# A decoder layer with mLSTM and memory attention on one core: weights of the last MLP chunk kept, memory input moved, root columns reordered, chunk steps spread, sums moved

## The chip, the cores and the metric

The kernel runs on one core of a Trainium2 chip. TensorE (PE in the profile) multiplies matrices; VectorE (DVE), ScalarE (ACT) and GpSimd (POOL) work element by element; SyncE (SP) issues the DMA transfers. Each engine takes its instructions in the order in which they stand in its queue and waits for semaphores that the others set. The metric is the time of one execution on the device in microseconds (us): the median of several runs.

## The reference

The input x has 1024 tokens of width 1024, the memory has 256 rows. One layer is computed, then a last RMSnorm (gains, weights and biases are parameters):

```
h     = rms_norm(x, norm_mix0)
qk, v, o_pre, i_pre, f_pre, q_mem = split(h @ w_in)      # 768, 768, 768, 4, 4, 256 columns
q, k  = split(silu(causal_conv4(qk, w_conv)))            # 4 heads of 96
y_ml  = rms_norm(mlstm(q, k, v, i_pre + b_i, log_sigmoid(f_pre + b_f)), w_hnorm) * sigmoid(o_pre)
mem_k, mem_v = split(rms_norm(mem, mem_norm) @ w_mem_kv)
y_mem = softmax(q_mem @ mem_k^T / 8) @ mem_v             # 4 heads of 64, 256 memory rows
x     = x + concat(y_ml, y_mem) @ w_out
x     = x + square(relu(rms_norm(x, norm_ffn0) @ w_ff1)) @ w_ff2   # 4096 hidden
out   = rms_norm(x, final_norm)
```

The mLSTM keeps a matrix state C for each head (96 x 192) and runs in chunks of 128 tokens with stabilised exponential gates: in a chunk, n = (q k^T * weights) v + q C; then C = decay * C + (k * u)^T v.

## The kernel before

**Products.** Every operand of a product in float32 is split into a high part of fewer bits and a low part, the rest. A product is three matmuls into the same PSUM bank (mm3, L110 high by high, L111 high by low, L112 low by high). `load_w` (L93) brings a weight: SP's DMA into a raw tile (4 of them), a cast on ACT for the high part (L88 or L91), a subtraction on POOL for the low part (L103). The results lie in a ring "w" of 5, or in another pool if one is given.

**Stages.** The tokens go in two halves (512 each), with d_model on the partitions. The work is written as Python generators: `run(dense, side, every)` issues a step of the dense work, and after every `every`-th step one step of the side work. L681 to L692 hold the plan: project_qk(0) (768 columns over 8 blocks of input) with the zeros of the memory's block matrices beside it; project_v(0) (two halves of four token tiles, 8 blocks each) with `memory_load`, which loads, scales, splits and squares the memory's rows (tile xm); then the query of the memory, the memory's keys and values (`memory_kv`), with the gates of the mLSTM beside it; project_o(0) with the memory's scores (tiles: softmax quotients pr L597, transposed by PE as ct L607); then project_qk(1) and project_v(1) with the chunks of the first half (`mlstm_chunk`, two yields each: s, k; n, c; the rest) after every second step; and so on.

**Roots.** An RMSnorm's sum of squares over partitions is a product with a matrix of ones (ssq, L142); two transpositions on DVE (L144, L150) with POOL's power between give the inverse roots as a row for each token (rr), and `rms_cols` copies them as a column (rk, four copies on DVE, L188). After project_qk's products DVE evacuates their banks with the factor rr (L285); convolutions follow (ACT L243, DVE L246, ACT L253 as tile ct, DVE L254).

**MLP.** Most of it runs in pairs of blocks with sums of weights. The last quarter of w_ff2 is direct, `last_chunk` (L1218): pass 0 makes 8 output blocks for the first half of the tokens (512 columns), two more passes make them for 256 tokens each of the second half (tok1, tok2). Every block is added to the residual (L1241), squared on ACT (L1244) and its square added on DVE (L1247, kept for the next block by `lag`). `root_first` sums them over partitions by PE (L159), and begins the root with ACT; `root_last` ends it on DVE; `write` multiplies and stores.

**What sets the order.** A scheduler with a simulated timeline orders each engine's queue when the kernel is built, within the data's dependences and the buffers; `keep_in_program_order` and `issue_after` bind single instructions. So the code's order moves what stands ahead of what on an engine, and the order in the queues has to be read from the built program.

## Time and profile before

| what | value |
|---|---|
| median of 3 runs | 1064.99 us (1062.97 to 1065.62) |
| profiled execution: its own time | 1062.4 us |
| its span, first to last instruction | 1060.7 us |
| mean granted TensorE clock | 0.993 |
| busy: PE, DVE, ACT, POOL | 1035.6, 696.7, 545.5, 592.7 us (98, 66, 51, 56%) |
| HBM read, written | 114.52, 36.19 MB, 142 GB/s over the span |

The busy time of an engine is the time in which one of its instructions ran. PE has hardly any free time in the whole span; the other three have much, but not in every stage. A row of a timeline has the start, the duration, the engine, the line, the operation, the output and its inputs, the count where rows of one kind are joined, and in brackets the idle time just before and what ended it.

### The profile page before, as it was taken

To read this page: it belongs to the slowest core of one execution; us is meant where nothing else is said; L and a number is where in the kernel's file an instruction comes from. 1 tells how busy PE (TensorE), PEld (TensorE's weight loads), DVE (VectorE), ACT (ScalarE), POOL (GpSimd) and SP (SyncE) were. 2 spreads that over 40 slices of the span, in tenths; PEclk is the share of its full clock that TensorE was granted. 3 is DMA by queue.
4 is the path that set the end of the run, shared out by engine and by line. 5 is a ranking of instruction groups with operands and counts; after the bars stand their busy time and mean duration, and the time that the engine had idled before them with its cause. 6 is when DMAs were issued, how large, how long until landed. Compare 5 with 4: busy or idle time off the path is not lost.

```text
span 1060.7 us, 14584 instructions
## 1 busy us (share of the span) xinstructions
PE 1035.6 (98%) x5018; PEld 887.1 (84%) x5018; DVE 696.7 (66%) x1122; ACT 545.5 (51%) x1050; POOL 592.7 (56%) x448
## 2 busy tenths in 40 slices
PE   9989999999999999999999999999999999999996
PEld 7988998899998888877888888887778888888885
DVE  6596885952766457996534433434899888878557
ACT  7464773344754354465665565555454433443273
POOL 6755435554424475004755566565568787776455
PEclk9999999999999999999999999999999999999999
DMA  7443333232324466326555453437775545544124
GB/s 223 115 126 109 115 122 87 69 93 89 99 60 120 151 190 196 100 65 215 198 186 184 155 189 134 172 120 239 258 212 174 158 142 167 152 137 139 54 78 158
DMA packets 81802, 152.46 MB, mean 144 GB/s; under 512 B 8096, under 2 KB 26560, under 8 KB 80192
## 3 DMA queue, kind: packets, MB, share of 16 engines
q1 hardware_dynamic: 81584, 151.51, 45.5%
q8 instruction: 39, 0.64, 0.3%
q14 instruction: 35, 0.29, 0.1%
q10 hardware_dynamic: 144, 0.03, 0.0%
HBM read 114.52 MB, written 36.19 MB: 142 GB/s over the span
## 4 chain that ended last, share of the span: by engine, by line
PE 73%; DVE 8%; DMA 6%; issue 5%; POOL 5%; ACT 3%; SPq 0%; DVEq 0%; POOLq 0%; ACTq 0%
PE fX L110 5%; PE fX L112 5%; PE fX L111 5%; DMA hr<-hd 4%; PE gX L112 3%; PE gX L111 3%; PE gX L110 3%; PE wo L110 3%; PE wo L112 3%; PE wo L111 3%; PE fZ L111 2%; PE fZ L110 2%; PE fZ L112 2%; PE o L110 2%; PE o L111 2%
## 5 line engine op out<-in xcount | busy, mean ns | idle before, releaser
L116 DVE TENSOR_TENSOR hb<-hr,hb 128x1024 fp32r<-128x1024 f32 x53 | 88.5, 1670 | 9.1 <-ACT hb L115 8.9
L1142 DVE TENSOR_TENSOR xo<-xo,gX 128x512 f32<-128x512 f32 x112 | 74.3, 682 | 26.9 <-PE gX L112 22.8
L111 PE MATMUL gX<-hb,w_b 128*128 128x512 f32 x224 | 87.3, 390 | 1.6 <-DVE hb L116 1.6
L110 PE MATMUL gX<-hb,w_b 128*128 128x512 f32 x224 | 86.4, 391 | 0.5 <-ACT hb L115 0.4
L112 PE MATMUL gX<-hb,w_b 128*128 128x512 f32 x224 | 85.5, 391 | 1.0 <-POOL w_b L797 1.0
L91 ACT ACTIVATE w_b<-S_b 128x512 fp32r<-128x512 f32 x56 | 34.9, 628 | 75.4 <-PE gX L112 33.5
L115 ACT ACTIVATE hb<-hr 128x1024 fp32r<-128x1024 f32 x53 | 55.8, 1053 | 32.4 <-DMA hr<-hd 32.0
L103 POOL TENSOR_TENSOR w_wo<-r_wo,w_wo 128x512 fp32r<-128x512 f32 x32 | 45.4, 1425 | 48.4 <-ACT w_wo L91 47.0
L797 POOL TENSOR_TENSOR w_b<-r_b,w_b 128x512 fp32r<-128x512 f32 x42 | 68.5, 1644 | 5.9 <-ACT w_b L91 5.9
L748 POOL TENSOR_TENSOR S_b<-r_b,r_b 128x512 f32<-128x512 f32 x28 | 44.9, 1605 | 32.7 <-DVE w_b L797 27.1
L797 POOL TENSOR_TENSOR w_a<-r_a,w_a 128x512 fp32r<-128x512 f32 x30 | 39.4, 1312 | 38.3 <-ACT w_a L88 37.5
L103 POOL TENSOR_TENSOR w_v<-r_v,w_v 128x388 fp32r<-128x388 f32 x32 | 39.5, 1245 | 31.9 <-ACT w_v L91 31.8
L103 POOL TENSOR_TENSOR w_o<-r_o,w_o 128x384 fp32r<-128x384 f32 x32 | 33.5, 1054 | 41.2 <-ACT w_o L91 41.2
L103 POOL TENSOR_TENSOR w_qk<-r_qk,w_qk 128x384 fp32r<-128x384 f32 x32 | 38.5, 1218 | 26.8 <-ACT w_qk L91 26.8
L110 PE MATMUL fX<-xa,w_a 128*128 128x512 f32 x128 | 50.1, 391 | 1.5 <-ACT hq L1004 1.2
L111 PEld LDWEIGHTS gX<-hb,w_b 128*128 128x128 f32 x224 | 42.1, 188 | 10.8 <-DVE hb L116 2.2
L110 PE MATMUL wo<-xa,w_wo 128*128 128x512 f32 x128 | 51.0, 400 | 0.0
L112 PEld LDWEIGHTS gX<-hb,w_b 128*128 128x128 f32 x224 | 42.1, 188 | 10.5 <-POOL w_b L797 1.8
L110 PEld LDWEIGHTS gX<-hb,w_b 128*128 128x128 f32 x224 | 41.9, 188 | 10.6 <-DVE xo L1142 1.0
L111 PE MATMUL wo<-xa,w_wo 128*128 128x512 f32 x128 | 50.1, 391 | 0.0
L112 PE MATMUL wo<-xa,w_wo 128*128 128x512 f32 x128 | 50.0, 390 | 0.0
L111 PE MATMUL fX<-xa,w_a 128*128 128x512 f32 x128 | 49.9, 389 | 0.0
(396 smaller groups left out, 3450.2 us busy)
## 6 DMA issues: line engine op xcount, KB each, us to landing
hr<-hd SPq DMA_DIRECT2D x53, 512.0 KB, 3.7
r_b<-w_ff SPq DMA_DIRECT2D x56, 256.0 KB, 3.0
hd<-hq SPq DMA_DIRECT2D x54, 256.0 KB, 2.0
hd<-hq SPq DMA_DIRECT2D x12, 1024.0 KB, 4.1
r_a<-w_ff SPq DMA_DIRECT2D x36, 256.0 KB, 2.7
r_wo<-w_out SPq DMA_DIRECT2D x32, 256.0 KB, 2.7
r_a<-w_ff SPq DMA_DIRECT2D x13, 512.0 KB, 4.6
r_v<-w_v SPq DMA_DIRECT2D x32, 194.0 KB, 2.4
```

Source lines behind the costliest of these rows:

```text
L91: st["first_part"] = A.activation(dst, src, AF.Copy).ins
L103: i = engine.tensor_tensor(w[:, 1, :n], raw[:, :n], w[:, 0, :n], ALU.subtract)
L110: keep(T.matmul(out, lhsT=lh, rhs=rh, start=start, stop=False, skip_group_check=goes_on))
L111: keep(T.matmul(out, lhsT=lh, rhs=rl, start=False, stop=False, skip_group_check=goes_on))
L112: keep(T.matmul(out, lhsT=ll, rhs=rh, start=False, stop=stop, skip_group_check=goes_on))
L115: A.activation(hi, src, AF.Copy)
L116: V.tensor_tensor(lo, src, hi, ALU.subtract)
L748: i = (on or (V if both is not None and sums_on_v and key != "S4" else G)).tensor_tensor(t, x, y, op)
L797: low = engine.tensor_tensor(w[:, 1], src, w[:, 0], ALU.subtract)
L1142: V.tensor_tensor(x, x, banks[e], ALU.add)
```

## The change

The change has five parts. (1) `memory_load` moves from project_v(0) to project_qk(0), where its steps alternate with those of the zeros (a new generator `turns`), from the sixth step on; project_v(0) runs alone, and the first weight of the memory's query is no longer loaded ahead. (2) In `memory_kv` the four copies of the root as a column are issued behind the last subtraction that makes the keys. (3) The first half's chunks take a step after every third step of project_qk(1), then after every second of project_v(1). (4) In `last_chunk` the weights are loaded and split once, in pass 0, and kept for the second half's passes; those of output blocks 4 to 7 lie in the pool of the squared activations. (5) In the pass tok2 the squares of blocks 4 to 7 are not added on DVE, but go one by one into PE's sum; the sum for tok1 is issued between the products of block 4 and of block 5.

```diff
--- before.py
+++ after.py
@@ -211,6 +211,16 @@
     def seq(*gens):
         for g in gens:
             yield from g
+
+    def turns(*gens):
+
+        gens = list(gens)
+        while gens:
+            for g in list(gens):
+                if next(g, gens) is gens:
+                    gens.remove(g)
+                else:
+                    yield
 
 
     att = ExitStack()
@@ -342,21 +352,13 @@
                     f()
             yield
 
-    def query_weight(h, b, u):
-        return load_w(a["w_qm"][b, u], 512, f"qm{h}{b}{u}")
-
-    def query_ahead():
-
-        st["qm_w", 0, 0, 0] = query_weight(0, 0, 0)
-        yield
-
     def project_qmem(h):
         qm = mem.tile([P, 2, 2, HT], F32R, tag="qm", name=f"qm{h}")
         st["qm", h] = qm
         for b in range(2):
             p = ps(f"qm{h}{b}")
             for u in range(2):
-                w = st.pop(("qm_w", h, b, u), None) or query_weight(h, b, u)
+                w = load_w(a["w_qm"][b, u], 512, f"qm{h}{b}{u}")
                 for kk in range(4):
                     k = 4 * u + kk
                     c = slice(kk * P, (kk + 1) * P)
@@ -410,8 +412,7 @@
                     mm3(p[:, :NMEM], w[:, 0, cc], w[:, 1, cc], xm[:, k, 0], xm[:, k, 1], k == 0, k == KB - 1)
                 if (b, u) == (1, 0):
                     parts = wpool.tile([P, 2, 512], F32R, tag="w", name="sums_m", bufs=5)
-                    rbc, c = rms(acc, NMEM, "m", [parts[:, i] for i in range(2)])
-                    rk = rms_cols(c, NMEM, "m")
+                    rbc, cols = rms(acc, NMEM, "m", [parts[:, i] for i in range(2)])
                 yield
         for b, p in enumerate(pk):
             t = at.tile([P, HT], F32, tag="cacc", name=f"mkt{b}", bufs=2)
@@ -420,7 +421,8 @@
                 rows = slice(64 * e, 64 * e + 64)
                 own = slice(NMEM * e, NMEM * e + NMEM)
                 A.activation(kbd[rows, b, 0, own], t[rows, :NMEM], AF.Copy)
-                V.tensor_tensor(kbd[rows, b, 1, own], t[rows, :NMEM], kbd[rows, b, 0, own], ALU.subtract)
+                keys_made = V.tensor_tensor(kbd[rows, b, 1, own], t[rows, :NMEM], kbd[rows, b, 0, own],
+                                            ALU.subtract).ins
         pv = [ps(f"mv{t}") for t in range(2)]
         for u in range(4):
             w = load_w(a["w_mv"][u], 512, f"mv{u}")
@@ -433,6 +435,8 @@
                         k == 0, k == KB - 1)
             if u < 3:
                 yield
+        with tc.issue_after(keys_made):
+            rk = rms_cols(cols, NMEM, "m")
         for t in range(2):
             s = at.tile([P, HT], F32, tag="cacc", name=f"mvt{t}", bufs=2)
             V.tensor_scalar(s[:, :NMEM], pv[t][:, :NMEM], rk[:, t:t + 1], None, ALU.mult)
@@ -678,13 +682,15 @@
 
     chunks = lambda h: seq(*(mlstm_chunk(h, t) for t in range(TPH)))
 
-    run(project_qk(0), seq(wait(3), memory_zeros()))
+    run(project_qk(0), seq(wait(5), turns(memory_load(), memory_zeros())))
     nc.sync.dma_start(gbias, a["gbias"].partition_broadcast(P))
     nc.sync.dma_start(whn, a["whn"].partition_broadcast(P))
-    run(project_v(0), seq(memory_load(), wait(4), query_ahead()))
+    run(project_v(0))
     run(seq(project_qmem(0), memory_kv()), seq(wait(3), gates(0)))
     run(project_o(0), tiles(0))
-    run(seq(project_qk(1), project_v(1)), chunks(0), every=2)
+    steps = chunks(0)
+    run(project_qk(1), steps, every=3, finish=False)
+    run(project_v(1), steps, every=2)
     rest = seq(gates(1), tiles(1), chunks(1))
     run(seq(project_qmem(1), project_o(1, lambda k: transpose_y(0, k))), rest, finish=False)
     run(project_out(0, lambda k: transpose_y(1, k)), rest)
@@ -1268,16 +1274,17 @@
                     keep(i)
             nc.sync.dma_start(out[h, :, b:b + 2, tok], o)
 
-        def weights(h, b):
+        def weights(b):
+
             for j in range(2):
-                ws[b, j] = load_w(a["w_ff2"][c, b // 2 % 2, b // 4, j], 512, f"f2{b}{j}{h}", fp if h and b > 3 else None)
+                ws[b, j] = load_w(a["w_ff2"][c, b // 2 % 2, b // 4, j], 512, f"f2{b}{j}", fp if b > 3 else None)
 
 
         tok = slice(0, HT)
         acc = cm.tile([P, HT], F32, tag="acc", name="oacc0")
         for b in range(KB):
             if b % 2 == 0:
-                weights(0, b)
+                weights(b)
             p = ps(f"f2{b}0")
             products(0, b, tok, p, 0)
             add(x1[0][:, b, tok], p, acc, b == 0, f"0{b}")
@@ -1287,7 +1294,6 @@
         tok1 = slice(0, HQ)
         acc1 = cm.tile([P, HT], F32, tag="acc", name="oacc1")
         for b in range(0, KB, 2):
-            weights(1, b)
             p = ps(f"f2{b}1")
             for e in range(2):
                 products(1, b + e, tok1, p, e * HQ)
@@ -1309,26 +1315,36 @@
         tok2 = slice(HQ, HT)
         acc2 = cm.tile([P, HT], F32, tag="acc", name="oacc2")
         late = []
+
+        def add_last(x, p, nm):
+
+            keep(V.tensor_tensor(x, x, p, ALU.add))
+            sq = fp.tile([P, HT], F32, tag="sum", name=f"sq_o2{nm}", bufs=3)
+            flat = sq[:, :HQ] if len(x.shape) == 2 else sq.rearrange("p (e t) -> p e t", e=2)
+            A.activation(flat, x, AF.Square)
+            late.extend([sq[:, :HQ]] if len(x.shape) == 2 else [sq[:, :HQ], sq[:, HQ:]])
+
         for b in range(0, KB - 2, 2):
             p = ps(f"f2{b}2")
-            for e in range(2):
-                products(1, b + e, tok2, p, e * HQ)
+            products(1, b, tok2, p, 0)
             if b == 4:
                 part = root_first([(ones, acc1[:, :HQ])], HQ, "o1")
-            add(x1[1][:, b:b + 2, tok2], p.rearrange("p (e t) -> p e t", e=2), acc2, b == 0, f"2{b}")
+            products(1, b + 1, tok2, p, HQ)
+            x, halves = x1[1][:, b:b + 2, tok2], p.rearrange("p (e t) -> p e t", e=2)
+            if b < 4:
+                add(x, halves, acc2, b == 0, f"2{b}")
+            else:
+                add_last(x, halves, b)
+                flush()
             scale(1, [b, b + 1], tok2)
             if b == 0:
                 keep(V.tensor_tensor(acc1[:, :HQ], acc1[:, :HQ], acc1[:, HQ:], ALU.add))
         r1 = root_last(part, HQ, "o1")
         write(1, 0, tok1, r1, G)
-        flush()
         for b in (KB - 2, KB - 1):
             p = ps(f"f2{b}2")
             products(1, b, tok2, p, 0)
-            x = x1[1][:, b, tok2]
-            keep(V.tensor_tensor(x, x, p[:, :HQ], ALU.add))
-            late.append(fp.tile([P, HT], F32, tag="sum", name=f"sq_o2{b}", bufs=3)[:, :HQ])
-            A.activation(late[-1], x, AF.Square)
+            add_last(x1[1][:, b, tok2], p[:, :HQ], b)
         write(1, 2, tok1, r1, V)
         part = root_first([(ones, s) for s in [acc2[:, :HQ], acc2[:, HQ:], *late]], HQ, "o2")
         scale(1, [KB - 2, KB - 1], tok2)
```

How this moves instructions is seen at three places of the built program. The numbers behind names are buffers; they differ between the two programs where more or fewer tiles were made before.

On ACT, in project_v(0) (w_v: a cast of a weight; ca and ct: steps of a convolution; v: the first half's evacuations; sq_m: squares of the memory), before:

```order
L91 ACTIVATE w_v_743<-r_v_741 128x388
L309 ACTIVATE v_434<-v_442,rk_x_389 128x2x192
L309 ACTIVATE v_436<-v_443,rk_x_389 128x2x192
L309 ACTIVATE v_438<-v_444,rk_x_389 128x2x192
L309 ACTIVATE v_440<-v_445,rk_x_389 128x2x192
L91 ACTIVATE w_v_760<-r_v_758 128x388
L253 ACTIVATE ct_538<-ca_532 128x512
L128 ACTIVATE sq_m_559<-xm_526 128x512
L91 ACTIVATE w_qm_777<-r_qm_775 128x512
L253 ACTIVATE ct_568<-ca_562 128x512
L243 ACTIVATE ca_595<-qk_114,small 128x512
L91 ACTIVATE w_v_782<-r_v_780 128x388
```

and of the change:

```order
L91 ACTIVATE w_v_743<-r_v_741 128x388
L319 ACTIVATE v_470<-v_478,rk_x_389 128x2x192
L319 ACTIVATE v_472<-v_479,rk_x_389 128x2x192
L263 ACTIVATE ct_559<-ca_553 128x512
L319 ACTIVATE v_474<-v_480,rk_x_389 128x2x192
L263 ACTIVATE ct_586<-ca_580 128x512
L319 ACTIVATE v_476<-v_481,rk_x_389 128x2x192
L91 ACTIVATE w_v_760<-r_v_758 128x388
L253 ACTIVATE ca_607<-qk_114,small 128x512
L253 ACTIVATE ca_634<-qk_114,small 128x512
L91 ACTIVATE w_v_777<-r_v_775 128x388
```

The cast of w_v_760 stood ahead of both ct; now it is behind them. The squares and casts of the memory and the cast of w_qm are gone from here, and the three casts behind w_v_760 stand close together.

On DVE, where the memory's roots are made (gaT: gates, copied and scanned; rr_m, rk_m: the memory's roots as row and column; mkt, kbd: keys), before:

```order
L470 COPY gaT_1053<-ga_1051 16x128
L150 STREAM_TRANSPOSE rr_m<-rc_m 128x256
L188 COPY rk_m<-rc_m 32x2 x4
L471 SCALAR_TENSOR_TENSOR gaT_1053<-gaT_1053 16x128
L418 TENSOR_TENSOR mkt_1020<-mk_926,rr_m 128x256
L418 TENSOR_TENSOR mkt_1026<-mk_961,rr_m 128x256
L129 TENSOR_TENSOR acc_1657<-acc_1657,sq_x_1693 128x512
L423 TENSOR_TENSOR kbd<-mkt_1020,kbd 64x256 x2
```

and of the change:

```order
L474 COPY gaT_1048<-ga_1046 16x128
L150 STREAM_TRANSPOSE rr_m<-rc_m 128x256
L475 SCALAR_TENSOR_TENSOR gaT_1048<-gaT_1048 16x128
L419 TENSOR_TENSOR mkt_1015<-mk_926,rr_m 128x256
L419 TENSOR_TENSOR mkt_1021<-mk_961,rr_m 128x256
L129 TENSOR_TENSOR acc_1657<-acc_1657,sq_x_1693 128x512
L424 TENSOR_TENSOR kbd<-mkt_1015,kbd 64x256 x2
L424 TENSOR_TENSOR kbd<-mkt_1021,kbd 64x256
L481 COPY gbp_917<-gp_1087 128x16
L424 TENSOR_TENSOR kbd<-mkt_1021,kbd 64x256
L188 COPY rk_m<-rc_m 32x2 x4
```

The scan now follows L150 directly, and the four copies rk_m stand behind the keys.

On PE, in the first half's chunks (c: the state's products of a chunk, two banks, two heads each; n: the chunk's output; s: its scores; qk, v: dense products of the second half), before, two uses of the pair of banks c and all that is between:

```order
L548 MATMUL c_2103<-v_438,uk_2039 96x193
L548 MATMUL c_2104<-v_438,uk_2039 96x193
L525 MATMUL s_2176<-qk_114 128x128 x4
L111 MATMUL qk_1951<-xa,w_qk_2205 128x512
L112 MATMUL qk_1951<-xa,w_qk_2205 128x512
L110 MATMUL qk_1952<-xa,w_qk_2205 128x512
L111 MATMUL qk_1952<-xa,w_qk_2205 128x512
L112 MATMUL qk_1952<-xa,w_qk_2205 128x512
L110 MATMUL qk_1953<-xa,w_qk_2205 128x512
L111 MATMUL qk_1953<-xa,w_qk_2205 128x512
L112 MATMUL qk_1953<-xa,w_qk_2205 128x512
L548 MATMUL c_2103<-v_438,uk_2039 96x193
L548 MATMUL c_2104<-v_438,uk_2039 96x193
```

and of the change the end of what stands between the pairs, from the 18th matmul behind the first pair on (the 18 are value products too):

```order
L110 MATMUL v_2165<-w_v_2276,xa 128x388
L111 MATMUL v_2165<-w_v_2276,xa 128x388
L112 MATMUL v_2165<-w_v_2276,xa 128x388
L110 MATMUL v_2162<-w_v_2340,xa 128x388
L111 MATMUL v_2162<-w_v_2340,xa 128x388
L112 MATMUL v_2162<-w_v_2340,xa 128x388
L552 MATMUL c_2222<-v_474,uk_2133 96x193
L110 MATMUL v_2163<-w_v_2340,xa 128x388
L111 MATMUL v_2163<-w_v_2340,xa 128x388
L112 MATMUL v_2163<-w_v_2340,xa 128x388
L110 MATMUL v_2164<-w_v_2340,xa 128x388
L552 MATMUL c_2223<-v_474,uk_2133 96x193
```

Between the first use of each bank and the second stood eight query-key products and the scores; now 21 value products stand ahead of the one bank, and 25 ahead of the other.

## Rows read from the trace of the kernel before

**Rows 1.** PE's waits over the span: us in total, times, longest.
```profile
PE v L111 <- POOL w_v L103: 2.5, 2, 1.7
PE c L548 <- DVE C L552: 1.9, 1, 1.9
PE ssq_o L159 <- DVE oacc L1247: 1.9, 1, 1.9
PE gp L476 <- DVE gaT L471: 1.7, 1, 1.7
...
PE v L110 <- ACT w_v L91: 1.1, 1, 1.1
```

**Rows 2.** Windows: length, busy us per engine (instructions); clock, DMA share, GB/s.
```profile
76.00:78.00 2.00, 2.00 (x9) 2.00 (x8) 1.44 (x1) 1.90 (x4) 1.56 (x2) 0.57 0.61 167
78.00:80.00 2.00, 2.00 (x7) 1.65 (x6) 0.95 (x5) 2.00 (x5) 1.85 (x2) 0.58 0.84 221
104.00:106.00 2.00, 2.00 (x11) 2.00 (x11) 1.87 (x6) 1.24 (x3) 0.00 (x0) 0.50 0.79 252
106.00:108.00 2.00, 2.00 (x10) 2.00 (x9) 0.62 (x2) 1.79 (x7) 1.88 (x2) 0.75 0.76 166
206.00:208.00 2.00, 1.99 (x8) 1.92 (x9) 2.00 (x6) 1.34 (x3) 1.18 (x3) 0.50 0.02 4
208.00:210.00 2.00, 2.00 (x10) 2.00 (x9) 2.00 (x4) 0.42 (x1) 1.74 (x1) 0.65 0.00 0
```

**Rows 3.** Windows of two stages: value projection's start, first half's chunks.
```profile
39.00:58.00 19.00, 19.00 (x110) 19.00 (x109) 18.49 (x33) 9.51 (x19) 9.72 (x8) 1.00 0.34 94
183.00:212.00 29.00, 26.79 (x136) 23.22 (x135) 28.06 (x62) 12.65 (x32) 14.99 (x13) 0.94 0.24 66
```

**Rows 4.** ACT's timeline, late project_v(0): start, us, instruction [idle before, releaser].
```profile
64.56 0.62 ACT L253 ACTIVATE ct<-ca 128x512 f32<-128x512 f32 x1
...
71.50 0.63 ACT L253 ACTIVATE ct<-ca 128x512 f32<-128x512 f32 x1 [2.81 <-DVE ca L246]
...
72.56 0.51 ACT L91 ACTIVATE w_v<-r_v 128x388 fp32r<-128x388 f32 x1
```

**Rows 5.** The page, costliest groups: POOL's lows of w_v (busy, mean ns, idle before).
```profile
L103 POOL TENSOR_TENSOR w_v<-r_v,w_v 128x388 fp32r<-128x388 f32 x32 | 39.5, 1245 | 31.9 <-ACT w_v L91 31.8
```

**Rows 6.** Tile xm, normalized memory input: durations in ns min/median/max.
```profile
L120 DVE SCALAR_TENSOR_TENSOR xm<-xm,small,xm x8: 473/476/477, 44.9 to 71.3; 128x256 fp32r<-128x256 f32 x8
...
DMA to landing us min/median/max: 2.6/3.0/3.2
```

**Rows 7.** DVE's timeline: root of the input, root columns, quotients of softmax.
```profile
38.92 0.71 DVE L150 STREAM_TRANSPOSE rr_x<-rc_x 128x512 f32<-128x512 f32 x1 [3.03 <-POOL rc_x L148]
39.56 1.69 DVE L188 COPY rk_x<-rc_x 32x4 f32<-32x4 f32 x4
41.28 3.68 DVE L285 TENSOR_TENSOR qk<-qk,rr_x 128x512 f32<-128x512 f32 x6
...
98.76 3.49 DVE L188 COPY rk_m<-rc_m 32x2 f32<-32x2 f32 x4
...
114.76 1.79 DVE L597 TENSOR_SCALAR pr<-pr,cst 128x256 f32<-128x256 f32 x2
```

**Rows 8.** SP's issues, end of project_qk(0): the sixth and the seventh w_v.
```profile
33.76 0.33 SPq L96 DMA_DIRECT2D r_v<-w_v  x1
...
35.81 0.33 SPq L96 DMA_DIRECT2D r_v<-w_v  x1
```

**Rows 9.** PE's timeline: first value product, a later one, ct, tail's sum.
```profile
38.88 0.34 PE L110 MATMUL v<-w_v,xa 128*128 128x388 f32 x1
...
66.44 0.33 PE L110 MATMUL v<-w_v,xa 128*128 128x388 f32 x1
...
116.57 0.60 PE L607 MATMUL ct<-ident,pr 128*128 128x128 f32 x4
...
1050.29 1.10 PE L159 MATMUL ssq_o<-oacc,ones 128*128 128x256 f32 x4 [1.85 <-DVE oacc L1247]
```

## The prediction

> **What bounds the kernel now.** I read the busy times first: TensorE (PE) works for 98% of the span, so the change can save only what PE loses. Two views show what it loses. The table of PE's waits has a few short ones at single places [rows 1]. The 2 us windows have the granted clock, and there a second loss stands behind the three larger waits: after PE stood, the windows that follow run at 0.50 to 0.75 [rows 2], towards the lower level of 1.2 GHz, where most of the span runs at 2.4. A wait of 1 to 2 us at these places costs about as much again in clock. Last I read the windows by stage for the engine that has no room beside PE: VectorE (DVE) is busy 18.49 of 19 us where the value projection starts, and 28.06 of 29 us in the chunk stage [rows 3]. Where DVE is full, what stands in its queue ahead of the instruction that PE needs sets PE's wait.
>
> **Stage 1, the value projection project_v(0).** PE waits 2.5 us in two pieces for the low part of a w_v and 1.1 us for a high part [rows 1], and the two windows behind run at 0.57 and 0.58 [rows 2], which loses 2 x (0.43 + 0.42) = 1.7 us. The cause stands in ACT's timeline: the tanh of a convolution, ct, starts at 71.50 after 2.81 us of waiting for DVE, and the cast of w_v stands behind it on ACT at 72.56 [rows 4]; POOL's low part comes behind that cast, as most of POOL's idle time at w_v does [rows 5]. DVE is late since the memory's input runs through it in this stage. The change takes that out: of eight lows at 0.476 us [rows 6], 3.8 us, six stood ahead of that ct, 2.9 us. The projection's own 16 weight loads keep their sequence. I count all of it as gone: 2.5 + 1.1 + 1.7 = **5.3 us**.
>
> What takes its place is of two kinds. (a) The memory's four loads, its casts, squares and sums now lie in project_qk(0). On DVE, two lows and three adds of squares now stand between L144 and L150 (the transpositions before and after the root), where it had 3.03 us of idle time, waiting for POOL [rows 7]. Two lows at 0.476 and three adds as long as L150's 0.71 would about fill the gap, 3.1, but the last piece comes late: its load stands on SP behind the sixth w_v load, which went out at 33.76, the seventh at 35.81 [rows 8], and wants the buffer of the piece two before it. I put it at 35.4. It lands after 3.0 [rows 6]; then two casts (0.476 each by the lows), a square (0.62 as ct, of the same 512 columns [rows 4]) and an add (0.71) give 40.7, against 38.92 for L150 before. So the evacuations of the query-key banks, from 41.28 on at 0.61 each [rows 7], start about 1.8 later, and the first is done at 43.7. PE begins the value products at 38.88 [rows 9], with two free banks; at 110 matmuls in 19 us [rows 3], 0.173 each, it wants a third bank after 26 of them, at 43.4. I take 0.5 us, from 0 (the load goes out right behind the sixth) to 1.6 (L150 moves by all 3.1), and 1.7 more if the clock falls.
>
> (b) On ACT the cast of the fourth weight of the second half now stands behind two ct, where it was ahead of both. The second of them ended at 64.56 + 0.62 = 65.2 [rows 4]; less the relief on DVE and with its later start, 65.2 - 2.9 + 1.8 = 64.1. With a cast of 0.51 and a low of 1.25, the mean [rows 5], the weight is whole at 65.9. PE wants it 12 matmuls before the product at 66.44 [rows 9], so at 64.4. That would be 1.5; part of the relief may come sooner, and I take 1.0, from 0 to 1.6, plus 1.7 of clock. The w_qm that is no longer fetched ahead is in this range: it stands behind the next two ct in the same way.
>
> **Stage 2, the memory's roots.** PE waits 1.7 us at gp for gaT [rows 1]: on DVE the scan that makes gaT stands behind the four copies rk_m, 3.49 us from 98.76 [rows 7]. The change puts the scan ahead of them, so it ends before PE arrives. The two windows behind the wait run at 0.50 and 0.75 [rows 2], 2 x (0.5 + 0.25) = 1.5. Together **3.2 us**. The copies do not vanish; they stand behind the halves of the keys, and the products mvt wait for them. What is late next: the quotients pr end at 114.76 + 1.79 = 116.55 [rows 7], and the transposition ct that reads them starts at 116.57 [rows 9], without slack. PE now comes 3.2 sooner, less 7 rows by which ct stands later in its queue (1.2), so at 114.6. If DVE keeps its pace there, PE waits 116.55 - 114.6 = 2.0; if DVE follows PE wholly, nothing. DVE has the scan and what hangs on PE's gp sooner, so I let it follow by 1.2. I take 0.8, from 0 to 2.0, plus 1.7 of clock at worst.
>
> A page speaks here. The four copies rk_m took 0.87 each, at a time when POOL ran lows of w_o without a pause [rows 7]; the four copies rk_x, of twice the columns, took 1.69 in all. The Trainium skill, "SBUF — State Buffer", section "SBUF: two separate sides", says that VectorE and GpSimd share a pair of ports under an exclusive lock: of two instructions that want it, one waits for the whole of the other. The trace fits that. By the rule the copies, now beside an almost idle POOL, take half as long, and the 0.8 goes to 0. It also speaks against the change: the memory's lows have both inputs in SBUF and would meet POOL's lows of w_qk in the first projection, so that (a) becomes 1.5 in place of 0.5. The two nearly cancel (0.2 worse).
>
> **Stage 3, the first half's chunks.** PE waits 1.9 us at c for C [rows 1], a bank that DVE's update has to clear, and the windows behind run at 0.50 and 0.65 [rows 2]: 2 x (0.5 + 0.35) = 1.7, together **3.6 us**. Before, eight query-key products (1.8 us) stood between the first pair of c products and the second. Now this chunk step lies in project_v(1), and 21 value products at 0.173, 3.6 us, stand between: about the 1.8 + 1.9 that was needed. I take 0.5 for what remains, from 0 to 2.0 (all of the wait again).
>
> **Last chunk.** Eight loads, eight casts on ACT and eight lows on POOL go. They lay beside PE's products, and none of PE's waits of 1 us or more is for a w_f, so I count nothing. The weights of blocks 4 to 7 now come in pass 0 and take slots of the pool of the squared activations, which earlier steps free; -0.5 to 0.6.
>
> **Tail.** Before the last root PE waits 1.9 us for a sum on DVE [rows 1], whose queue holds the adds of squares; then four matmuls sum for 1.10 us [rows 9], and four more. The change makes these eight twelve and needs no add on DVE: 1.9 - 1.1 = 0.8, less 0.1 for the last square; **0.7** (0.4 to 1.0). What follows stays: roots, multiplications, stores.
>
> **Sum.** 5.3 + 3.2 + 3.6 + 0.7 = 12.8 gained, less 0.5 + 1.0 + 0.8 + 0.5 = 2.8 of new waits: 10.0. The profiled execution took 1062.4 around its span of 1060.7, so it would take 1052.4. The median of the three runs, 1064.99, lies 2.6 above that execution, and I forecast **1055.0 us**.
>
> **The rivals.** *C, all these waits go and none comes.* 12.8, so 1052.2. For it: (a) and (b) are within 1.5 us of nothing. Against: three places without slack.
> *B, the waits move.* DVE has the same work in all, and PE comes sooner to the next thing that DVE makes. If (a), (b) and ct all come late, each with its clock, (1.0 + 1.7) + (1.3 + 1.7) + (2.0 + 1.7) = 9.4 returns, and stage 3's 0.5; 2.9 stays: 1062.1. For it: DVE busy 18.49 of 19 us. Against: each needs its own delay.
> *D, slower.* In project_v(1) every second step takes a chunk's step, and DVE has the C updates, the scaling of the hidden state and the second half's convolutions in one queue. If at each of four chunk steps its work between n and C is longer than the 3.6 us that PE has between, the 1.9 + 1.7 = 3.6 comes four times, 14.4 in place of 3.6. The other stages give 9.2 less 2.3 = 6.9, the chunks lose 10.8: net 3.9 slower, 1068.9. It decides from 3.6 us on. For it: DVE busy 28.06 of 29 us [rows 3]. Against: with every third step in project_qk(1) the chunks lie farther apart than before.
>
> **How the numbers follow.** The forecast has 47%, with its own range 1051.5 to 1058; C 25%, B 20%, D 8%. About 0.3%, 3.2 us, is what a measurement of this kernel can tell from no change. The forecast and C are faster; B lies at that edge, and I halve it; D is slower. So faster 0.82, same 0.10, slower 0.08. The range goes down to C from the fastest of the executions shown, 1062.4 - 12.8 = 1049.6, and up to B with the 0.6 by which the slowest run lies above the median, 1062.7; D and the worst part of B stay outside.
>
> **What would show it.** In the profile after: no wait of PE for w_v near 73, none at gp, no 1.9 at c or ssq_o, and a clock of 1.00 in the windows that are at 0.50 to 0.75 now. If (a) comes, PE waits at v near 43 for an evacuation; if (b), near 64 for w_v; if the third, at ct for pr near 114. I am wrong if PE's waits in project_v(1) are several above 1.5 us, or if the waits go and the time stays; then the clock fell for another cause than these waits.

## The result, and the profile after

The changed kernel took 1053.06 us (median of 6 runs, 1051.36 to 1055.76) against 1064.62 us for the kernel before (6 runs, 1062.97 to 1067.73): ratio 0.9892, 95% interval 0.9872 to 0.9913, where 1055.0 was forecast. In two later comparisons, on two different chips, the same two kernels gave 0.9915 (0.9900 to 0.9931) and 0.9925 (0.9907 to 0.9943). The span of the profiled execution fell from 1060.7 to 1049.6 us.

PE's waits in the profile after (us in total, times, longest), the lines that answer to [rows 1]:

```profile
PE ct L611 <- DVE pr L601: 1.6, 3, 0.6
PE k L535 <- DVE wt L530: 1.4, 1, 1.4
PE v L110 <- DVE qk L295: 1.2, 1, 1.2
PE gX L111 <- DVE hb L116: 1.2, 1, 1.2
...
PE v L111 <- POOL w_v L103: 0.3, 1, 0.3
```

The waits at gp, at c and at ssq_o are gone, and those for w_v but for 0.3. New are 1.2 at v for an evacuation, 1.6 at ct in three pieces (0.2 before), and 1.4 at k (0.3 before).

The windows that answer to [rows 2], and those behind the wait at k (columns as there):

```profile
76.00:78.00 2.00, 2.00 (x11) 1.63 (x10) 1.23 (x5) 1.46 (x4) 2.00 (x3) 1.00 0.67 184
78.00:80.00 2.00, 2.00 (x10) 1.66 (x9) 1.72 (x2) 1.56 (x3) 2.00 (x2) 1.00 0.68 215
104.00:106.00 2.00, 2.00 (x13) 2.00 (x13) 1.18 (x6) 2.00 (x8) 0.76 (x2) 1.00 0.41 117
106.00:108.00 2.00, 2.00 (x13) 2.00 (x12) 2.00 (x4) 0.21 (x1) 1.94 (x2) 1.00 0.45 122
196.00:198.00 2.00, 2.00 (x8) 2.00 (x7) 2.00 (x4) 0.86 (x2) 0.00 (x0) 0.50 0.47 140
198.00:200.00 2.00, 2.00 (x10) 2.00 (x9) 2.00 (x5) 0.48 (x1) 0.00 (x0) 0.68 0.00 0
```

The first four, at 0.50 to 0.75 before, have the full clock. The pair behind the wait at k is low, as the pair behind c was.

DVE's timeline where the wait at v arises [rows 7] (start, us, instruction, idle time before):

```profile
39.72 1.65 DVE L120 SCALAR_TENSOR_TENSOR xm<-xm,small,xm 128x256 fp32r<-128x256 f32 x2 [1.53 <-ACT xm L119]
41.30 1.50 DVE L129 TENSOR_TENSOR accm<-accm,sq_m 128x512 f32<-128x512 f32 x1
42.73 0.70 DVE L150 STREAM_TRANSPOSE rr_x<-rc_x 128x512 f32<-128x512 f32 x1
43.36 0.64 DVE L188 COPY rk_x<-rc_x 32x4 f32<-32x4 f32 x4
44.03 3.68 DVE L295 TENSOR_TENSOR qk<-qk,rr_x 128x512 f32<-128x512 f32 x6
```

PE's row that waits for the first of these evacuations:

```profile
44.77 0.45 PE L110 MATMUL v<-w_v,xa 128*128 128x388 f32 x1 [1.23 <-DVE qk L295]
```

And DVE's at the memory's roots:

```profile
94.67 0.85 DVE L475 TENSOR_TENSOR_SCAN gaT<-gaT 16x128 f32<-16x128 f32 x1
...
100.99 0.68 DVE L188 COPY rk_m<-rc_m 32x2 f32<-32x2 f32 x4
```

The lows of the memory's last piece began at 39.7, and L150 moved from 38.92 to 42.73. PE wanted the bank at 43.5 and had it at 44.8. The scan now runs ahead of the four copies rk_m, and these took 0.68 in their new place, 3.49 before. What POOL did beside these copies, before:

```profile
98.05 1.29 POOL L103 TENSOR_TENSOR w_mv<-r_mv,w_mv 128x512 fp32r<-128x512 f32 x1
99.30 2.92 POOL L103 TENSOR_TENSOR w_o<-r_o,w_o 128x384 fp32r<-128x384 f32 x3
```

and in the changed kernel:

```profile
99.15 1.02 POOL L103 TENSOR_TENSOR w_o<-r_o,w_o 128x384 fp32r<-128x384 f32 x1 [0.25 <-ACT w_o L91]
102.07 1.20 POOL L103 TENSOR_TENSOR w_o<-r_o,w_o 128x384 fp32r<-128x384 f32 x1 [1.90 <-ACT w_o L91]
```

Before, POOL had no pause beside the copies; now it stands from 100.2 to 102.07, and all four copies lie in that gap.

The sum for the last root on PE [rows 9]:

```profile
1037.99 1.03 PE L159 MATMUL ssq_o<-oacc,ones 128*128 128x256 f32 x4
1038.85 1.90 PE L159 MATMUL ssq_o<-sq_o,ones 128*128 128x256 f32 x8
```

Twelve matmuls now run without a wait: 4 and then 8.

To find where the time went I cut each trace at the first matmul of a dense product, by the starts in PE's timeline: the value projection, the query, the keys, the second half's query, the MLP's first product (fX), the last chunk's first (f), and the end of its last. Two profiles of the kernel before (the second is e9) and three of the changed one (after, e5, e12), in us:

| stretch | before | changed | forecast of the difference |
|---|---|---|---|
| value projection to the keys | 50.89, 50.88 | 46.88, 46.44, 49.33 | -3.8 |
| keys to the second query (roots, scores, chunks) | 156.21, 156.81 | 153.77, 153.95, 153.48 | -2.4 and -3.1 |
| MLP up to the last chunk | 575.36, 573.98 | 572.07, 574.53, 573.35 | none |
| products of the last chunk | 53.23, 53.25 | 52.62, 52.62, 52.63 | 0 |
| from there to the end | 12.25, 12.23 | 11.46, 11.44, 11.45 | -0.7 |

By the means this is -3.3, -2.8, -1.4, -0.6 and -0.8. The order of instructions in the MLP is the same in both programs on every engine by the traces; its stretch differs from execution to execution by up to 2.5 us of the same kernel. Without it the change gives some 7.5 us.

### The profile page after: what moved, and what is told of

Its sections match the earlier page's. It is cut to its first block, busy times and chain, and to the rows that moved or that the text cites. A ratio compares the mean times of both kernels' runs of the same rounds, so it can differ in the third digit from the quotient of the medians.

```text
span 1049.6 us, 14545 instructions
## 1 busy us (share of the span) xinstructions
PE 1031.6 (98%) x5022; PEld 885.2 (84%) x5022; DVE 695.4 (66%) x1121; ACT 542.5 (52%) x1042; POOL 580.4 (55%) x440
## 4 chain that ended last, share of the span: by engine, by line
PE 77%; DVE 7%; DMA 6%; issue 4%; POOL 3%; ACT 2%; SPq 0%; DVEq 0%; POOLq 0%; ACTq 0%
PE fX L112 5%; PE fX L110 5%; PE fX L111 5%; PE gX L110 4%; DMA hr<-hd 4%; PE gX L112 4%; PE gX L111 4%; PE wo L110 3%; PE wo L111 3%; PE wo L112 3%; PE fZ L111 3%; PE fZ L112 3%; PE fZ L110 3%; PE gZ L112 2%; PE gZ L111 2%
## 5 line engine op out<-in xcount | busy, mean ns | idle before, releaser
L116 DVE TENSOR_TENSOR hb<-hr,hb 128x1024 fp32r<-128x1024 f32 x53 | 86.4, 1629 | 9.6 <-ACT hb L115 9.5
L103 POOL TENSOR_TENSOR w_v<-r_v,w_v 128x388 fp32r<-128x388 f32 x32 | 36.8, 1163 | 45.7 <-ACT w_v L91 45.5
L103 POOL TENSOR_TENSOR w_o<-r_o,w_o 128x384 fp32r<-128x384 f32 x32 | 35.8, 1127 | 39.5 <-ACT w_o L91 37.0
L110 PE MATMUL fX<-xa,w_a 128*128 128x512 f32 x128 | 50.0, 390 | 0.2 <-ACT hq L1020 0.2
L91 ACT ACTIVATE w_b<-r_b 128x512 fp32r<-128x512 f32 x42 | 26.4, 628 | 45.8 <-PE gX L112 27.9
```

What stands on the lines that cost most here:

```text
L91: st["first_part"] = A.activation(dst, src, AF.Copy).ins
L103: i = engine.tensor_tensor(w[:, 1, :n], raw[:, :n], w[:, 0, :n], ALU.subtract)
L110: keep(T.matmul(out, lhsT=lh, rhs=rh, start=start, stop=False, skip_group_check=goes_on))
L116: V.tensor_tensor(lo, src, hi, ALU.subtract)
```

## The experiments

All are compared with the kernel before on their own chip. The kernels e1 to e4 ran on one chip, e5 to e8 on another, e9 to e12 on a third; the changed kernel's own ratio differs by 0.003 between the three comparisons, so that differences of 2 us are read from the stretches of the trace. A stretch is one execution, and a low clock behind a single wait can change it by 1.5 to 1.7 us.

**e1, the memory's input back in its old place.**

```diff
-    run(project_qk(0), seq(wait(5), turns(memory_load(), memory_zeros())))
+    run(project_qk(0), seq(wait(3), memory_zeros()))
-    run(project_v(0))
+    run(project_v(0), memory_load())
```

> The changed kernel with the memory's input back in project_v(0) (old place, the query's weight still not fetched ahead). Theory A (each part pays in its own stage): PE's waits for w_v near 66 to 76 and the low clock behind them return, the start of the memory's query goes from 74.7 back to near 78.1, and the time rises by some 3.5 us, to a ratio near 0.9925 against the kernel before. Rival B (the waits only move, the parts carry each other): the wait at v for the evacuation near 43 goes (1.2 us) and w_v's waits return only in part; under 1.5 us slower than the changed kernel, ratio near 0.990. The stretch from the first fX to the first product of the last chunk, whose order is the same in all kernels, took 575.4 before and 572.1 after: if that is scatter from execution to execution it lies anywhere from 571.5 to 576 here, if the change makes it, it is 572.1 within 0.5.

Measured: 1052.02, ratio 0.9912 (0.9896 to 0.9929). Value projection to the keys 46.93, like the changed kernel's 46.88; no wait for any w_v, and one of 1.6 for the query's own weight. Theory A fell: moving the memory's input is not what took the waits away. The other edit of that part is the weight that is no longer fetched ahead.

**e2, the root columns at once.**

```diff
                     rbc, cols = rms(acc, NMEM, "m", ...)
+                    rk = rms_cols(cols, NMEM, "m")
...
-        with tc.issue_after(keys_made):
-            rk = rms_cols(cols, NMEM, "m")
```

> The changed kernel with the four root columns copied at once, ahead of the scan. Theory A: PE's wait of some 1.7 us at gp and the clock of 0.5 to 0.75 behind it return, the wait of 1.6 us at ct in three pieces goes; net 2 to 3 us slower, ratio near 0.9915. Rival B: the copies take only 0.2 each in this place, since POOL's work lies otherwise by now, and the wait does not return; within 0.7 us of the changed kernel, ratio near 0.989.

Measured: 1055.34, ratio 0.9942 (0.9921 to 0.9963). Keys to the second query 156.17, 2.4 more than the changed kernel's mean of 153.73: theory A in the size. The wait at gp is back, by PE's waits of e2:

```profile
PE ct L610 <- DVE pr L600: 2.5, 4, 0.8
PE gp L479 <- DVE gaT L474: 1.7, 1, 1.7
```

But the wait at ct did not go, as theory A had it; it is 2.5 in four pieces.

The copies are slow again; the tile rk_m (durations in ns, min/median/max) in e2:

```profile
L188 DVE COPY rk_m<-rc_m x4: 594/944/967, 95.5 to 98.0; 32x2 f32<-32x2 f32 x4
```

and in the changed kernel:

```profile
L188 DVE COPY rk_m<-rc_m x4: 156/159/165, 101.0 to 101.5; 32x2 f32<-32x2 f32 x4
```

The windows of e2 around the wait:

```profile
98.00:100.00 2.00, 0.51 (x3) 0.48 (x4) 1.96 (x5) 0.22 (x1) 0.96 (x2) 1.00 0.00 0
100.00:102.00 2.00, 2.00 (x17) 2.00 (x16) 1.94 (x6) 1.45 (x4) 0.00 (x0) 1.00 0.49 142
102.00:104.00 2.00, 2.00 (x13) 1.86 (x12) 1.30 (x4) 1.63 (x6) 1.03 (x2) 1.00 0.77 208
```

PE stands in 98:100, and the clock stays full behind it: the same wait that cost 1.5 of clock in [rows 2] cost none here. (Behind k this trace has a low clock, as one of the three profiles of the changed kernel has.)

**e3, the chunks as before.**

```diff
-    steps = chunks(0)
-    run(project_qk(1), steps, every=3, finish=False)
-    run(project_v(1), steps, every=2)
+    run(seq(project_qk(1), project_v(1)), chunks(0), every=2)
```

> The changed kernel with the chunks after every second step of both projections, as before. The chunk stage (second start of qk to second start of the query) took 91.7 before and 92.2 after by the two traces. Theory A' (the new plan only turned the wait at c into one at k): the stage takes 91.5 to 92.5, the time is within 0.7 us of the changed kernel, ratio near 0.989. Rival (the old plan beside the other parts would wait more, at c and behind it): 94 or more, the ratio near 0.9915.

Measured: 1054.28, ratio 0.9936 (0.9917 to 0.9954); second qk to second query 93.38, keys to the second query 154.83, 1.1 more than the changed kernel. Both expectations missed. They started from stages of 91.7 and 92.2 us that are not the same work: twelve products of the memory's attention (co) stand inside this stretch in the changed kernel and in e3, and ahead of it in the kernel before; in e3 they take 1.45 us. The wait at c (1.9) is back and the one at k gone. The clock behind c is low in e3 (windows at 0.50 and 0.68, 1.6 us), and behind k in one of the three profiles of the changed kernel, so that most of the 1.1 can be the clock: the new plan is worth 1 us at most.

**e4, the last chunk as before** (its function word for word from the kernel before).

> The changed kernel with the last chunk as before: weights loaded and split for each half, squares added on DVE. Theory A: from the last product on 0.8 us comes back and within the chunk 0.6, in all 1.0 to 1.5, ratio near 0.9905; PE waits 1.9 at ssq_o. Rival: the tail is set by roots and stores alone, nothing comes back, ratio 0.989.

Measured: 1055.57, ratio 0.9942 (0.9926 to 0.9958). Products of the last chunk 53.25, end 12.24: the 0.6 and the 0.8 come back, and PE waits 1.9 at ssq_o. Theory A; the further distance in time lies in the MLP's stretch (573.82) and in what scatters.

**e5, the changed kernel again.**

> The changed kernel once more, on the same chip as the next three, so that they can be compared with it. Ratio to the kernel before 0.987 to 0.991. The MLP stage (first fX to the first product of the last chunk), of the same order in all kernels, has taken 575.4 before, 572.1 after and 572.6 to 573.9 in the four experiments. If this is scatter, it will differ from 572.1 by some tenths to 2 us here; if it belongs to the changed kernel, it is 572.1 again.

Measured: 1054.04, ratio 0.9915, just above the expected range. The MLP's stretch is 574.53, 2.5 longer than in its first profile: scatter.

**e6, the kernel before without the fetch.**

```diff
-    run(project_v(0), seq(memory_load(), wait(4), query_ahead()))
+    run(project_v(0), memory_load())
```

> The kernel before with one edit: the first weight of the memory's query is not fetched ahead in project_v(0); the memory's input stays where it was. My prediction's cause (DVE late through the memory's lows) says that PE's 3.6 us of waits for w_v near 66 to 74 stay, for DVE has the same work: query start at 77 to 78, time within 0.7 us of before. The rival F, formed from e1 (the weight fetched ahead takes a place in the ring, and the last w_v is cast behind a ct for it): the waits for w_v go, the query starts near 73.5 with a wait of 1.5 for its own weight, the keys some 3.5 us sooner than before, ratio near 0.9967.

Measured: 1058.44, ratio 0.9957 (0.9941 to 0.9973), 4.6 us faster than before by this one edit. The query starts at 73.48, value projection to the keys 46.97. ACT's timeline, to be held against [rows 4]:

```profile
68.44 0.52 ACT L91 ACTIVATE w_v<-r_v 128x388 fp32r<-128x388 f32 x1
71.75 0.63 ACT L253 ACTIVATE ct<-ca 128x512 f32<-128x512 f32 x1 [2.79 <-DVE ca L246]
...
72.81 0.61 ACT L91 ACTIVATE w_qm<-r_qm 128x512 fp32r<-128x512 f32 x1
```

DVE is as late for ct as before, 2.79 us; but the last w_v is cast ahead of it, at 68.44, and what stands behind ct is the query's weight. Rival F holds; my prediction's cause does not.

**e7, the fetch put back into the changed kernel.**

```diff
-    run(project_v(0))
+    run(project_v(0), seq(wait(12), query_ahead()))
...
-                w = load_w(a["w_qm"][b, u], 512, f"qm{h}{b}{u}")
+                w = st.pop(("qm_w", h, b, u), None) or query_weight(h, b, u)
```

> The changed kernel (memory input in the first projection) with the query's first weight fetched ahead again from project_v(0). By my prediction's cause, the w_v waits stay away, since DVE has been relieved: within 0.7 us of the changed kernel. By F, the cast of the last w_v stands behind two ct again, and PE waits for it 1.5 us or more near 70 to 73, with a low clock behind: 2 to 4 us slower than the changed kernel.

Measured: 1055.43, ratio 0.9930 (0.9914 to 0.9946), 1.4 us above e5, not separable. The waits for w_v are back in part, and the query starts at 77.30. PE's waits of e7:

```profile
PE v L111 <- POOL w_v L103: 2.1, 3, 1.4
...
PE v L110 <- DVE qk L295: 1.3, 1, 1.3
```

POOL's:

```profile
67.19 1.64 POOL L103 TENSOR_TENSOR w_qm<-r_qm,w_qm 128x512 fp32r<-128x512 f32 x1 [0.72 <-ACT w_qm L91]
68.79 2.88 POOL L103 TENSOR_TENSOR w_v<-r_v,w_v 128x388 fp32r<-128x388 f32 x2
```

ACT's:

```profile
66.49 0.62 ACT L91 ACTIVATE w_qm<-r_qm 128x512 fp32r<-128x512 f32 x1
...
72.30 1.29 ACT L263 ACTIVATE ct<-ca 128x512 f32<-128x512 f32 x2 [4.35 <-DVE ca L256]
73.50 0.52 ACT L91 ACTIVATE w_v<-r_v 128x388 fp32r<-128x388 f32 x1
```

The query's low stands on POOL ahead of the next w_v's, which is what PE waits 1.4 for, and the last w_v is cast behind two ct again (0.45). The memory's input was out of DVE's way, and still PE waited: F in kind, with 2.1 us and no low clock, less than it expected. Moving the memory's input did lower these waits from 3.6 to 2.1, but PE waits 1.3 at v for an evacuation in its place: 3.4 us in all.

**e8, chunks after every fourth step, with e1.**

```diff
-    run(project_qk(1), steps, every=3, finish=False)
+    run(project_qk(1), steps, every=4, finish=False)
```

> A try at a better kernel: the changed one with the memory's input back in project_v(0) without the fetch (as e1) and the first half's chunks after every fourth step of project_qk(1), then every second of project_v(1). Theory A' (the head of DVE's queue sets k and c, and a wider spacing gives DVE time): the wait of 1.4 at k near 192 and its low clock go, the stage takes 89 to 90 in place of 91.5, ratio near 0.987. Rival (the steps only bunch up in project_v(1), where the chunk's step is then as dense as before): waits at c or k there, 92 or more, ratio 0.990 or above.

Measured: 1057.83, ratio 0.9952 (0.9938 to 0.9967). The wait at k goes, and four others come in project_v(1) (at v 0.5, s 1.1, n 1.3 and 1.4); the stage takes 94.16. The rival holds: waits at several chunk steps, the kind that my prediction's D named, at a wider spacing than the change has.

**e9, the kernel before again.**

> The kernel before, once more, with a profile. By scatter (the view formed from e1 to e8: MLP stage 572.1 to 574.5 at the same order, the clock behind the same wait low in one execution and full in the next), the MLP stage is not 575.4 again but some 573 to 575, and not all three of the low clocks (76 to 80, 104 to 108, 206 to 210) come again; PE's waits for w_v (3.6 us), at gp (1.7), at c (1.9) and at ssq_o (1.9) are there to a tenth or two. If the low clock belongs to these waits, as my prediction priced it, all three come again and cost 4.9 us.

Measured: 1064.09, one execution. The waits are there to a tenth; the clock is low behind w_v and behind gp, and full behind c. The MLP's stretch is 573.98. Scatter.

**e10, the chunk's weights one step earlier.** The m maximum, exponentials and mask become a function, called for the next chunk at the end of a chunk's first step:

```diff
+        if h == 0 and t < TPH - 1:
+            st["ahead", c + 1] = chunk_weights(h, t + 1)
         yield
         C = st.get("C")
```

> The changed kernel, with the exponential weights of the first half's next chunk (the m maximum on DVE, the exponentials on ACT, the mask on POOL) issued one step earlier. Theory H (PE's wait of 1.4 to 1.7 us at k near 193 comes since the weights are begun too late, behind the convolutions in DVE's queue): the wait at k goes, the chunk stage (second qk to second query) takes 89.5 to 90.5 in place of 91.5 to 92.2, ratio 0.2% better than the changed kernel's on this chip. Rival (DVE is full there, 27.3 of 29 us, so the wait moves to c, n or an evacuation): the stage stays at 91 to 92.5 and the time within 0.7 us of the changed kernel.

Measured: 1055.25, ratio 0.9927 (0.9907 to 0.9946), against 0.9925 for e12. The wait at k is 1.7, as in e12, and the stage takes 92.51, in e12 91.82 (e10 has a low clock there and e12 has none). DVE's timeline of e10 there:

```profile
190.66 1.49 DVE L516 TENSOR_TENSOR m<-m,mp 128x512 f32<-128x512 f32 x1 [0.36 <-DMA m<-pd]
...
193.82 0.58 DVE L588 SCALAR_TENSOR_TENSOR sc<-sc 128x4 f32<-128x4 f32 x1 [1.12 <-POOL sc L587]
194.33 0.68 DVE L539 SCALAR_TENSOR_TENSOR wt<-s,wt 128x512 f32<-128x512 f32 x1
```

The maximum (L516) still starts at 190.7, behind the same convolutions and for its DMA, and the wt that PE waits for stands behind an instruction that waits 1.12 for POOL. The scheduler left the instruction where it was, so that H is neither shown nor refuted. The rival's ground, a full DVE, does not hold at this place: DVE stands for 1.12 us. The first profile of the changed kernel has the same, and PE's products k start at 194.02 there:

```profile
192.78 0.58 DVE L577 SCALAR_TENSOR_TENSOR sc<-sc 128x4 f32<-128x4 f32 x1 [1.12 <-POOL sc L576]
193.28 0.68 DVE L530 SCALAR_TENSOR_TENSOR wt<-s,wt 128x512 f32<-128x512 f32 x1
```

and POOL's:

```profile
191.74 1.01 POOL L576 TENSOR_TENSOR sc<-sc,mhalf 128x4 f32<-128x4 f32 x1 [0.58 <-DVE sc L575]
192.71 0.64 POOL L520 TENSOR_SCALAR_AFFINE_SELECT wt<-wt 128x512 f32<-128x512 f32 x1
```

The root for the previous chunk's output (sc) stands on both engines ahead of the weights wt that PE needs: on POOL ahead of their mask (L520), on DVE ahead of their product with the scores (L530). No run put wt ahead of sc, so whether the wait at k goes with that is not shown.

**e11, the memory's last piece behind the evacuations as well.**

```diff
+            with tc.issue_after(st["evacuated", 0]) if k == KB - 2 else nullcontext():
                 for i in range(2):
                     split_scaled(...)
```

> As e10, and the low parts and the square's sum of the memory's last piece stand on DVE behind the evacuations of the first query-key banks. If (a) was right, the wait at v near 43 (0.8 to 1.2 us) goes and nothing comes for it: the query starts 0.8 to 1.2 us sooner than in e10, and the time is as much below. Rival: the evacuated banks were not what PE needed, the wait becomes one at w_v behind, gain under 0.3.

Measured: 1054.43, ratio 0.9921 (0.9899 to 0.9944). The wait at v falls from 1.3 in e10 to 0.7, the query starts at 74.61 (75.02 in e10), and the query's weight then waits 0.6. (a) had its cause right in part; POOL's root and the first sums still hold L150 until 41.66. Nothing was gained by it: value projection to the keys takes 47.22, in e10 46.99. The rival holds.

**e12, the changed kernel on that chip.**

> The changed kernel on the chip of e10 and e11, for comparison: ratio 0.988 to 0.992; the waits at v near 43, at ct and at k as in its two earlier profiles; the clock behind the wait at k low or full, by chance.

Measured: 1054.75, ratio 0.9925. The ratio lies just above the expected range. The wait at k is 1.7 with a full clock. Between 42 and 47 PE waits 1.2 for a w_v, which the two earlier profiles don't have, and 1.4 for the evacuation, and behind these the clock falls, to 0.54. No version tried is faster than the changed kernel beyond the measurement.

## Why the prediction was right, point by point

**Stage 1: size right, cause wrong.** The forecast was 3.8 less up to the keys, and 3.3 was measured (by the means). That the size came out is luck, for another edit made it. The failed step is "the memory's input runs through it in this stage. The change takes that out": e6 has the memory's input in place and loses the waits, e7 has it moved and keeps 2.1 of them, with 1.3 at the evacuation added. The weight fetched ahead is cast and split among the last w_v, and the last of these stands behind a ct that waits for DVE; without it they are cast ahead of that ct, though DVE is as late. That it takes one of the ring's five places and so sets the last w_v back by one is argued from the code alone. The order of before has the w_qm cast between those of w_v; I had counted its loss as a risk in (b), not as the gain. (a) was taken as 0.5 and came as 0.8 to 1.4 (1.2 in the first profile), inside its range, but not by its sum: L150 moved by 3.8 where 3.1 was the bound, and the copies rk_x behind it took 0.64 where they had taken 1.69, which gave back 1.05. (b) was taken as 1.0 and came as 0.3; the 1.2 for a w_v in e12 lies at another place.

**Stage 2: the wait right, the rest in part luck.** 2.4 forecast, 2.4 by e2, though e2 has no low clock behind gp, for which 1.5 was counted. The wait at gp of 1.7 went. At ct 0.8 was taken, and the three profiles have 1.6, 2.3 and 1.7, where the two of before have 0.2 and 0.8. The prediction made these waits the price of the earlier gp; but e2 has 2.5 and e6 2.0 there, with the wait at gp in place, so that PE's gain in stage 1 alone can bring them. The copies fell from 0.87 to 0.16 each; before, the longer ones took 0.94 to 0.97, as long as one of POOL's lows of w_o beside them (2.92 for three). So the Trainium skill's rule of the shared ports ("SBUF — State Buffer", section "SBUF: two separate sides") is borne out, further than the half I gave it. The wait at ct did not go to 0 with the short copies. The last piece's work on DVE, beside POOL's w_v lows, stretched too (L120 0.83 each, L129 1.50, where 0.48 and 0.7 were counted), as the rule's second half said.

**Stage 3: the step that failed.** "21 value products at 0.173, 3.6 us, stand between: about the 1.8 + 1.9 that was needed": at c that held, the wait is gone in all three profiles. But the term for what remains, 0.5, was too small: another matmul that needs DVE, k for wt, now waits 1.4 to 1.7, and the stage gained 1.1 at most (e3) in place of 3.1. This is rival B's "the waits move", at a place that B did not name.

**The clock term was too dear on the average.** I took 1.5 to 1.7 for each of the three waits, as the trace had it. Over all profiles the same wait has a low clock behind it in one execution and none in the next: behind gp low in both profiles of before, full in e2 and e6; behind c low in before and e3, full in e6 and e9; behind k low in after, e2, e7, e10 and e11, full in e1, e4, e5 and e12. Nine of these 17 waits paid it; the waits for w_v, the third place that I priced, paid it in both profiles of before. All runs carry their mean granted clock: on the two chips that ran both kernels it was 0.9924 (14 runs) and 0.9940 (11) before, 0.9968 and 0.9960 (6 each) with the change. Over some 1060 us that is, as an estimate, 4.7 and 2.1 us, net of what the new waits paid. So part of the 4.9 us came, and how much is chance.

**Last chunk and tail.** Taken as 0 and 0.7, measured 0.6 and 0.8. The 0.6 holds a wait for w_f that I had left out, 0.3 in the profile before and 0.4 in e4.

**The sum.** 10.0 was forecast; the stretches give 7.5 and the medians of the three comparisons 11.6, 9.1 and 8.0. Stages 2 and 3 together gave 2.8, where 5.5 was forecast. The first profile's 11.1 has 3.3 from the MLP, which no step named: two errors of about 3 us, what stages 2 and 3 lacked and the MLP's scatter, stood against each other there. That is luck.

## What to carry to other kernels

A weight fetched ahead into a ring need not be free: here it put the cast of the stage's last weight behind an instruction that waits, and that wait came to TensorE (3.9 us from the value projection to the keys, with the clock). Before a wait is put down to an engine's load, look at what else changed place in the queue that waits. And where a wait is removed, ask for the next instruction that reads from the same engine, and what stands ahead of its source in that queue: here 1.4 to 1.7 of the 1.9 us came back there, behind an instruction that itself waited for GpSimd.

## What the runs showed of the hardware

Whether TensorE's granted clock fell to the 1.2 GHz level behind a wait was not set by the kernel's order alone. The changed kernel's wait at k, in e5, on PE's timeline:

```profile
195.13 0.55 PE L535 MATMUL k<-ident,qk 96*128 96x96 f32 x4 [1.69 <-DVE wt L530]
```

and the two windows behind it:

```profile
196.00:198.00 2.00, 2.00 (x12) 2.00 (x13) 2.00 (x6) 0.00 (x0) 0.65 (x1) 1.00 0.48 133
198.00:200.00 2.00, 2.00 (x13) 2.00 (x12) 2.00 (x5) 1.44 (x3) 0.00 (x0) 1.00 0.22 70
```

1.69 us of waiting and a full clock; in the profile after, 1.39 and 0.50. What PE did before was the same: dense query-key products, then the wait, then small transpositions. The Trainium skill, "TensorE: Matmul & The Clock Gate", section "Part 1: The HAM clock gate", says that the chip's look at activity runs on by itself and does not begin with the kernel; that would make it a matter of phase, and no run here shows the phase. A low clock cost 1.5 to 1.7 us per wait where it came.
